# The first layer's first blocks: eight split products or sixteen whole float32 ones

## The chip, the core and the metric

The kernel runs on one core of one Trainium2 chip. The metric is the device time of one execution in microseconds (us); the times shown are those of three runs. TensorE has two clock levels, 1.2 and 2.4 GHz; the profile gives the share that was granted (1.0 is 2.4 GHz).

## What is computed

Two layers over 256 tokens of width 2048, all in float32. Each layer takes a modulation `mod = silu(c) @ w_ada + b_ada` (six vectors of 2048), then a mixer and a feed-forward:

```python
h = rmsnorm(x, g_pre_mix[i]) * (1.0 + sc1) + sh1
z = h @ w_in[i]                       # 2048 x 6608: GLA's q, k, v, g, a and RWKV7's r, k, v, w, a, g
o_gla = gla_mixer(...)                # 8 heads, causal decayed attention
o_rwkv = rwkv7_mixer(...)             # 16 heads, delta rule
y = jnp.concatenate([o_gla, o_rwkv], axis=-1) @ w_out[i]
x = x + gt1 * rmsnorm(y, g_post_mix[i])
h = rmsnorm(x, g_pre_ffn[i]) * (1.0 + sc2) + sh2
y = jnp.square(jax.nn.relu(h @ w_ff1[i])) @ w_ff2[i]
x = x + gt2 * rmsnorm(y, g_post_ffn[i])
```

## The kernel before

Channels lie on partitions: `x` and `h` are 16 k-tiles of 128 channels by 256 tokens. A weight block is 2048 inputs by 128 outputs, 1 MiB; `wtile` (L283) loads it into `wraw` (three buffers of 1 MiB) from SyncE's queue (SP), and `split` (L295) makes of each half two float32r parts: `hi` by a cast on ScalarE, `lo` by a subtraction on VectorE. `h` is split the same way into `hh` and `hl`. A block is then 16 k-tiles of three products (`hi` x `hh`, `hi` x `hl`, `lo` x `hh`), 48 in all (L311 to L313), each 128x128 weights by 256 columns. Smaller products in the mixers are whole float32 ones: one product each of undivided operands.

The modulation is 96 jobs per layer (`ada_job`, L251): load 1 MiB of `w_ada`, multiply by `silu(c)` and sum on VectorE (L256).

The first stage is `first_norm` (L357). For k-tile k it does the two jobs that its scale and shift need, makes `h` of that k-tile (`norm_block`, L434), loads `w8[k]` (the k-th k-tile of eight blocks, 512 KiB), splits it and adds 8 x 3 products (`grow`, L348) to eight accumulators, one in each of the eight PSUM banks. These eight blocks (`FIRST[0]`, L55) are the low-rank columns w, a, g, g and the keys k0 to k3.

Then `mixers` (L899 and on) runs the other blocks of `w_in` in the order of the words in `ORDER[0]` (L68): `kab` two key blocks, `qn` a query and a key block of GLA, `hn` its values, `gn` its gates, `vn` RWKV's r and v of pair n; `T` posts the inverse of the 32 x 32 diagonal blocks (`inverse32`, L605), which needs all keys. Words post chains of dependent small work (`Chains`, L106): at most two are active, and after each quantum (4 k-tiles of a block, 12 products) one step of them is put between. A word outside `EARLY` waits while more than one chain is queued. `v0`'s chain needs `T`; `vn` needs `v(n-2)`. The modulation jobs 32 to 79 are spread over the weight tiles: 48/58 a tile at first, none after the word `R0`, and after `Ra` the rest over 34 tiles, the last 16 of which are `w_out`'s. The banks are `psm` (3), `psx` (3) and `ps2` (a pair), and the first blocks hold all of them until their words are reached.

## Time and profile before

| | us |
|---|---|
| runs: median (lowest to highest) | 2786.74 (2786.28 to 2793.4) |
| span of the profiled execution | 2786.0 |
| TensorE busy in it | 2658.6 |
| VectorE busy in it | 1997.1 |
| ScalarE busy in it | 1421.5 |

The page gives the profiled execution by its span alone; the median of the runs is 0.7 us above it. Busy times of TensorE are those of overlapping records. The rows that are used stand below; times are us from the start of the span.

### The profile page before, as it was taken

Reading aid. Unit: us, or ns where it says so; the run is one execution under the profiler, and the core shown is the slowest. Engines: PE = TensorE matmul, PEld = TensorE weight load, DVE = VectorE, ACT = ScalarE, POOL = GpSimd, SP = SyncE. Lnnn points to the kernel's source line nnn. Section 1 sums busy time; section 2 is a strip of 40 time slices with the busy share of each in tenths; the row PEclk is TensorE's granted clock in tenths of the full one; section 3 lists DMA queues with packets and bytes.
Section 4 is the critical chain, followed back from the end, with each engine's and each line's share of the span. In section 5 each row is a group of like instructions: output and inputs, shape, how many; then the busy total and the mean of one; then the engine's idle time right before and its main releaser. Section 6 shows DMA issues by size and latency. Waiting matters only on the chain.

```text
span 2786.0 us, 55551 instructions
## 1 busy us (share of the span) xinstructions
PE 2658.6 (95%) x23388; PEld 2551.7 (92%) x23388; DVE 1997.1 (72%) x2961; ACT 1421.5 (51%) x2357; POOL 59.2 (2%) x153
## 2 busy tenths in 40 slices
PE   5689999999999999999999999999999999999997
PEld 4678888898999999999988889888989999999997
DVE  8997986678867777777777798655785465565655
ACT  3378644445644434434577875444474443443443
POOL 0000000000000000000001000000000000000000
PEclk8799999999999999999999999998999999999999
DMA  9775576576777777777745547654845666666653
GB/s 402 312 278 196 182 279 239 208 271 231 254 287 289 275 284 284 286 281 282 282 176 206 205 154 264 224 175 159 327 157 212 213 213 218 218 213 212 212 184 119
DMA packets 104082, 659.20 MB, mean 237 GB/s; under 512 B 11540, under 2 KB 20884, under 8 KB 32408
## 3 DMA queue, kind: packets, MB, share of 16 engines
q1 hardware_dynamic: 87848, 618.19, 61.5%
q10 hardware_dynamic: 15984, 37.46, 3.7%
q8 instruction: 183, 3.00, 0.4%
q14 instruction: 67, 0.55, 0.1%
HBM read 638.83 MB, written 16.78 MB: 235 GB/s over the span
## 4 chain that ended last, share of the span: by engine, by line
PE 84%; DVE 9%; DMA 3%; ACT 3%; issue 2%; ACTq 0%; POOL 0%; DVEq 0%; SPq 0%
PE pm L311 14%; PE pm L313 14%; PE pm L312 14%; PE px L312 8%; PE px L313 8%; PE px L311 8%; DVE raw L256 3%; DVE lo L300 2%; PE p L504 1%; DMA raw<-in_wout_dram 1%; PE pm L993 1%; PE pm L994 1%; PE px L451 1%; PE pm L995 1%; ACT hi L299 1%
## 5 line engine op out<-in xcount | busy, mean ns | idle before, releaser
L300 DVE TENSOR_TENSOR lo<-raw,hi 128x1024 fp32r<-128x1024 f32 (+1 forms) x792 | 959.7, 1216 | 544.3 <-ACT hi L299 537.8
L299 ACT CAST hi<-raw 128x1024 fp32r<-128x1024 f32 (+1 forms) x792 | 822.3, 1043 | 800.6 <-PE pm L312 356.1
L311 PE MATMUL pm<-hh,hi 128*128 128x256 f32 x2624 | 762.5, 291 | 3.6 <-ACT hi L299 1.5
L313 PE MATMUL pm<-hh,lo 128*128 128x256 f32 x2624 | 750.4, 286 | 3.9 <-DVE lo L300 3.9
L312 PE MATMUL pm<-hl,hi 128*128 128x256 f32 x2624 | 749.9, 286 | 0.0
L311 PEld LDWEIGHTS pm<-hh,hi 128*128 128x128 f32 x2624 | 504.5, 192 | 14.1 <-issue 2.0
L313 PEld LDWEIGHTS pm<-hh,lo 128*128 128x128 f32 x2624 | 504.9, 192 | 8.9 <-DVE lo L300 5.2
L312 PEld LDWEIGHTS pm<-hl,hi 128*128 128x128 f32 x2624 | 505.4, 193 | 4.6 <-issue 1.6
L256 DVE CUSTOM_DVE_ANT_0 raw<-raw,cond 128x2048 f32<-128x2048 f32 x192 | 439.0, 2287 | 38.3 <-DMA raw<-in_ada_dram 37.8
L313 PE MATMUL pm<-hid,lo 128*128 128x256 f32 x1024 | 289.0, 282 | 0.0
L313 PE MATMUL px<-hid,lo 128*128 128x256 f32 x1024 | 288.3, 282 | 0.0
L312 PE MATMUL px<-hid,hi 128*128 128x256 f32 x1024 | 288.2, 281 | 0.0
L312 PE MATMUL pm<-hid,hi 128*128 128x256 f32 x1024 | 288.0, 281 | 0.0
L311 PE MATMUL pm<-hid,hi 128*128 128x256 f32 x1024 | 287.2, 280 | 0.0
L311 PE MATMUL px<-hid,hi 128*128 128x256 f32 x1024 | 287.1, 280 | 0.0
L313 PE MATMUL px<-hh,lo 128*128 128x256 f32 x896 | 253.6, 283 | 0.0
L311 PE MATMUL px<-hh,hi 128*128 128x256 f32 x896 | 253.5, 283 | 0.0
L312 PE MATMUL px<-hl,hi 128*128 128x256 f32 x896 | 253.5, 283 | 0.0
L311 PEld LDWEIGHTS px<-hid,hi 128*128 128x128 f32 x1024 | 194.5, 190 | 0.0
L311 PEld LDWEIGHTS pm<-hid,hi 128*128 128x128 f32 x1024 | 194.4, 190 | 0.0
L313 PEld LDWEIGHTS pm<-hid,lo 128*128 128x128 f32 x1024 | 193.1, 189 | 0.0
L313 PEld LDWEIGHTS px<-hid,lo 128*128 128x128 f32 x1024 | 193.0, 189 | 0.0
(333 smaller groups left out, 4184.4 us busy)
## 6 DMA issues: line engine op xcount, KB each, us to landing
raw<-in_ff_dram SPq DMA_DIRECT2D x242, 1024.0 KB, 4.9
raw<-in_ada_dram SPq DMA_DIRECT2D x192, 1024.0 KB, 6.2
raw<-in_win_dram SPq DMA_DIRECT2D x90, 1024.0 KB, 5.1
raw<-in_wout_dram SPq DMA_DIRECT2D x32, 1024.0 KB, 5.4
raw<-in_ff1s_dram SPq DMA_DIRECT2D x16, 896.0 KB, 4.6
spill<-pk ACTq DMA_DIRECT2D x16, 640.0 KB, 4.1
pk<-spill ACTq DMA_DIRECT2D x16, 640.0 KB, 5.0
raw<-in_w_dram SPq DMA_DIRECT2D x16, 512.0 KB, 10.5
```

The source lines that it names most:

```text
L256: nc.vector.tensor_tensor_reduce(out=raw, in0=raw, in1=self.cond, op0=ALU.mult, op1=ALU.add, scale=1.0, scalar=0.0, accum_out=self.mod[:, ...
L299: self.nc.scalar.copy(hi, half)
L300: self.nc.vector.tensor_tensor(lo, half, hi.bitcast(F32), op=ALU.subtract)
L311: nc.tensor.matmul(ps, hi[:, n % 8], xh(k), start=n == 0, stop=False)
L312: nc.tensor.matmul(ps, hi[:, n % 8], xl(k), start=False, stop=False)
L313: nc.tensor.matmul(ps, lo[:, n % 8], xh(k), start=False, stop=n == KT - 1)
L451: self.nc.tensor.matmul(ps, self.ones, sq[:, q], start=k + q == 0, stop=k + q == KT - 1)
L504: self.nc.tensor.matmul(v[:, h, n + c], l[hs, cs], r[hs, cs], start=True, stop=True)
L993: nc.tensor.matmul(vps[c], hh[:, kk, cs], hi[:, kq], start=kk == 0, stop=False)
L994: nc.tensor.matmul(vps[c], hl[:, kk, cs], hi[:, kq], start=False, stop=False)
L995: nc.tensor.matmul(vps[c], hh[:, kk, cs], lo[:, kq], start=False, stop=kk == KT - 1)
```

## The change

`FIRST[0]` has sixteen blocks: w, g, g, a, q0's two, k0 to k7, q1's two. Each of the eight banks holds two of them, side by side (256 columns each). They are no longer split: the stage loads `w16[k]` (1 MiB: the k-th k-tile of sixteen blocks, into `wraw`) and multiplies it by `h` itself, one whole float32 product per block and k-tile. Only the first of a bank's two products of k-tile 0 carries the start flag. `hh` and `hl` are still made for the later blocks. `ORDER[0]` takes all of these words first, and `EARLY` names them. `f512`, which now holds `h` for TensorE, has three buffers in this stage; the masks are loaded into a buffer of the modulation's pool. The rest of the diff takes comments out.

```diff
-FIRST = ((WB_W, WB_A, WB_G, WB_G + 1) + tuple(range(WB_K, WB_K + 4)),
+FIRST = ((WB_W, WB_G, WB_G + 1, WB_A, WB_GLA, WB_GLA + 1) + tuple(range(WB_K, WB_K + 8)) + (WB_GLA + 6, WB_GLA + 7),
...
-ORDER = ('k01 k23 q0 h0 g0 k45 q1 k67 R0 h1 P.9 T g1 q2 h2 g2 q3 v0 Ra v1 v2 v3 v4 v5 v6 v7 h3 g3',
+ORDER = ('q0 k01 k23 k45 k67 q1 h0 g0 R0 h1 P.9 T g1 q2 h2 g2 q3 v0 Ra v1 v2 v3 v4 v5 v6 v7 h3 g3',
...
-EARLY = ("k01", "k23")
+EARLY = ("q0", "k01", "k23", "k45", "k67", "q1")
...
-        mf = self.wraw.tile([P, D], F32, name="raw")[:, 0:NMASK]
+        mf = pool.tile([P, D], F32, name="raw", bufs=PRE_BUFS)[:, 0:NMASK]
...
-        first = [self.psm.tile([P, 512], F32, name="pm") for _ in range(3)] + [self.bank() for _ in range(3)]
-        first += [pair[:, n] for n in range(2)]
-        self.first = [(ps[:, :T], True, True) for ps in first]
+        banks = [self.psm.tile([P, 512], F32, name="pm") for _ in range(3)] + [self.bank() for _ in range(3)]
+        banks += [pair[:, n] for n in range(2)]
+        self.first = [(ps[:, n * T:n * T + T], True, True) for ps in banks for n in range(2)]
         for k in range(KT):
             self.ada_job(0, k, pool)
             self.ada_job(0, 16 + k, pool)
-            self.norm_block(pool, 0, rstd, 0, k, 1)
+            h = self.norm_block(pool, 0, rstd, 0, k, 1)
             if k == KT - 2:
-                self.constants()
-            raw = pool.tile([P, D // 2], F32, name="raw8", bufs=3)
-            nc.sync.dma_start(out=raw, in_=self.a["w8"][k])
-            hi, lo = self.split(raw, P)
-            self.grow(hi, lo, self.hh[:, k], self.hl[:, k], k)
+                self.constants(pool)
+            raw = self.wraw.tile([P, D], F32, name="raw")
+            nc.sync.dma_start(out=raw, in_=self.a["w16"][k])
+            w = raw.rearrange("p (n c) -> p n c", c=P)
+
+            for n, (ps, _, _) in enumerate(self.first):
+                nc.tensor.matmul(ps, w[:, n], h[:, 0], start=k == 0 and n % 2 == 0, stop=k == KT - 1,
+                                 skip_group_check=True)
...
-        t = pool.tile([P, n, T], F32, name="f512")
+        t = pool.tile([P, n, T], F32, name="f512", **({"bufs": 3} if n == 1 else {}))
...
+        return t
```

## Rows read from the trace of the kernel before

**Rows 1.** The page's first part: busy us, share of the span, instructions.

```profile
PE 2658.6 (95%) x23388; PEld 2551.7 (92%) x23388; DVE 1997.1 (72%) x2961; ACT 1421.5 (51%) x2357; POOL 59.2 (2%) x153
```

**Rows 2.** Windows: stretch, its length, busy us (instructions) by engine, clock, DMA share, GB/s.

```profile
27.00:132.00 105.00, 69.54 (x383) 65.99 (x384) 101.97 (x166) 32.32 (x52) 3.45 (x1) 0.78 0.89 362
132.00:272.00 140.00, 127.37 (x1331) 116.54 (x1330) 121.31 (x265) 110.12 (x222) 8.74 (x26) 0.97 0.67 236
272.00:330.00 58.00, 52.70 (x606) 50.34 (x605) 51.31 (x130) 37.36 (x57) 2.26 (x6) 0.94 0.50 178
330.00:353.00 23.00, 21.86 (x308) 20.42 (x307) 22.03 (x54) 16.64 (x33) 0.00 (x0) 1.00 0.55 185
353.00:576.00 223.00, 220.88 (x2106) 191.04 (x2104) 155.90 (x216) 100.92 (x224) 11.29 (x18) 1.00 0.67 239
576.00:668.00 92.00, 90.20 (x736) 88.67 (x736) 73.03 (x81) 44.05 (x69) 4.33 (x16) 1.00 0.88 326
```

**Rows 3.** Timeline of VectorE, one k-tile of the first stage: start, duration, instruction.

```profile
98.50 1.23 DVE L300 TENSOR_TENSOR lo<-raw,hi 128x1024 fp32r<-128x1024 f32 x1
99.65 0.42 DVE L444 TENSOR_TENSOR hl<-f,hh 128x256 fp32r<-128x256 f32 x1
...
100.45 2.28 DVE L256 CUSTOM_DVE_ANT_0 raw<-raw,cond 128x2048 f32<-128x2048 f32 x1
...
105.68 1.23 DVE L300 TENSOR_TENSOR lo<-raw,hi 128x1024 fp32r<-128x1024 f32 x1
```

**Rows 4.** Windows of 10 us in the first stage, and SyncE's last issue for it.

```profile
50.00:60.00 10.00, 6.10 (x33) 5.78 (x34) 10.00 (x21) 3.92 (x6) 0.00 (x0) 0.66 1.01 417
...
120.00:130.00 10.00, 6.91 (x38) 6.54 (x39) 8.32 (x14) 4.15 (x7) 1.45 (x1) 0.79 0.06 15
...
106.94 0.33 SPq L372 DMA_DIRECT2D raw<-in_w_dram  x1
```

**Rows 5.** Timeline of TensorE in the first stage; in brackets the idle time before.

```profile
27.58 1.01 PE L353 MATMUL pm<-hh,hi 128*128 128x256 f32 x3 [8.63 <-ACT hh L443]
...
33.93 0.28 PE L353 MATMUL p<-hh,hi 128*128 128x256 f32 x1
...
40.58 1.01 PE L353 MATMUL pm<-hh,hi 128*128 128x256 f32 x3 [4.33 <-ACT hh L443]
...
132.06 0.41 PE L355 MATMUL p<-hh,lo 128*128 128x256 f32 x1
```

**Rows 6.** Timeline of TensorE around four float32 records, and line L518's count.

```profile
141.05 0.28 PE L312 MATMUL pm<-hl,hi 128*128 128x256 f32 x1
141.17 0.60 PE L518 MATMUL px<-th,wsmA 128*128 128x256 f32 x2
141.60 0.59 PE L519 MATMUL px<-al,wsmA 128*128 128x256 f32 x2
141.85 0.47 PE L313 MATMUL pm<-hh,lo 128*128 128x256 f32 x1
142.15 0.28 PE L311 MATMUL pm<-hh,hi 128*128 128x256 f32 x1
...
L518 PE MATMUL px<-th,wsmA x32: 377/379/483, 134.8 to 1581.2; 128*128 128x256 f32 x32
```

**Rows 7.** Groups by line, VectorE, 132 to 350 us: busy, mean ns, idle before.

```profile
L300 DVE TENSOR_TENSOR lo<-raw,hi 128x1024 fp32r<-128x1024 f32 x52 | 63.3, 1223 | 10.7 <-ACT hi L299 10.6
L256 DVE CUSTOM_DVE_ANT_0 raw<-raw,cond 128x2048 f32<-128x2048 f32 x11 | 25.1, 2285 | 2.3 <-DMA raw<-in_ada_dram 2.3
```

**Rows 8.** Four lines, 0 to 640 us: duration min/median/max in ns, first and last start.

```profile
L596 DVE COPY_PREDICATED at<-masks,p x8: 731/736/749, 156.1 to 270.2; 128x512 f32<-128x512 uint8 x8
L618 DVE STREAM_TRANSPOSE o<-o x1: 2111/2111/2111, 275.9 to 275.9; 128x1024 f32<-128x1024 f32 x1
L640 DVE STREAM_TRANSPOSE tn<-o x1: 2032/2032/2032, 325.9 to 325.9; 128x1024 f32<-128x1024 f32 x1
L654 PE MATMUL px<-tn,at x64: 191/191/212, 353.4 to 537.6; 32*32 32x32 f32 x64
```

More of the change, by code (lines that the diff above doesn't have):

```diff
@@ L214, in setup, with constants @@
         self.vmix = self.dram.tile([8, P, T], F32, name="vmix")
-    def constants(self):
+    def constants(self, pool):
         nc = self.nc
@@ L1180, in _pack @@
     a["win"] = np.stack([_pack_win(f["w_in"][i], f["vres_w_down"][i - 1] if i else None) for i in range(L)])
-    a["w8"] = a["win"][0][list(FIRST[0])].reshape(8, P, KT, P).transpose(2, 1, 0, 3).reshape(KT, P, 8 * P)
+    a["w16"] = a["win"][0][list(FIRST[0])].reshape(16, P, KT, P).transpose(2, 1, 0, 3).reshape(KT, P, 16 * P)
     a["wins"] = _by_k(a["win"][1][list(FIRST[1])])
```

## Prediction

> **What bounds the kernel now.** I read the page first: TensorE is busy for 95% of the span, VectorE for 72% [rows 1]. Matmul records overlap, so this doesn't say how full TensorE is; the starts of consecutive records do. Then I cut the touched part into stages [rows 2]: 27 to 132 us is the first stage (modulation, first blocks); 132 to 353 us is the part of the first layer's mixers up to the first `v` pair (I call it stage A); then the `v` pairs, and from 576 us `w_out`. Everything after 668 us is left as it is.
>
> The first stage is paced by VectorE: busy 102.0 of 105 us [rows 2], with one k-tile every 7.18 us (from one `lo` row to the next: 98.50, 105.68) [rows 3]. A k-tile costs it two reductions of 2.28, one `lo` of 1.23, two passes of 0.42 and small ones. The DMA runs full beside it (417 GB/s, share 1.01) until the 16th weight tile is issued at 106.94; then it has nothing left of this stage (share 0.06 from 120 to 130) [rows 4]. TensorE works in bursts with gaps, at a mean granted clock of 0.78 [rows 2].
>
> In stage A no engine is at its end all the time. VectorE is the fullest: 121.3 + 51.3 + 22.0 = 194.6 of 221 us, 88% [rows 2]. TensorE's need is less than its busy time: a quantum of 12 products is 12 x 0.12 = 1.43 us (0.12 from one start to the next, 141.05 to 141.17 [rows 6]). Up to `v0` there are 104 quanta = 149 us, with some 27 us of small float32 products (an estimate from the shapes and the 0.215 below): 80% of 221. The chain through it: the last key block's mask at 270.2, the 32 x 32 inverse from its first transpose at 275.9 to its last at 325.9, the first use of its result at 353.4 [rows 8].
>
> **First stage, after.** Per k-tile, VectorE loses one `lo` (1.23): 7.18 - 1.23 = 5.95 us. ScalarE loses one cast. `hh` and `hl` are still made. So VectorE no longer paces it.
>
> DMA: a k-tile brings 2 MiB of modulation and now 1 MiB of weights, 3.15 MB; at 417 GB/s [rows 4] 7.5 us. The whole stage moves 53 MB (33.6 modulation, 16.8 weights, 2.1 `x`, constants), 127 us, with the start some 130 us. The mixers then load 8 MiB less, so the kernel's bytes stay the same.
>
> TensorE: a whole float32 product leaves two records; the 16 products of L518 show as 32 [rows 6]. Price: after the product at 141.05 (whose 0.12 ends at 141.17) come four such records, one split product (0.12), and the next starts at 142.15: (142.15 - 141.17 - 0.12) / 4 = 0.215 a record, 0.43 a product, each with weights of its own. At half clock the price doubles (0.41 against 0.28 are the durations at the two levels [rows 5]). A k-tile: 16 x 0.43 = 6.9 us at 2.4 GHz, against 24 x 0.12 = 2.9 before. The block itself gets dearer: 16 x 0.43 = 6.9 us whole, 48 x 0.12 = 5.7 us split; the saving is of splits and of place, not of TensorE's work.
>
> The Trainium skill, "FP8 and Floating Point Precision", TensorE Precision Notes, says that true FP32 takes four passes through the array. Were each pass priced as one split product, a product would cost 0.48 and a k-tile 7.6 us, the stage would end some 11 us later, and the result would be about 2771; two records of 0.215 say 0.43, and the row decides.
>
> So DMA (7.5) and TensorE (6.9) are close. TensorE starts at 27.6 as now. The first burst ran at half clock until about 33.9 [rows 5], which loses 3 us; then 16 x 6.9: 27.6 + 3 + 110 = 141. By the DMA: last bytes at 130, then reduction, small passes, `h` (some 4 us), the last 16 products 6.9: 141 too. Now the last one starts at 132.06 [rows 5]. Extension: +8.5 us, bounds +6 to +15.
>
> New waits: SP's load of `w16[k]` waits for a buffer of `wraw`, which is now free only when TensorE is through with `w16[k-3]`; queued behind it on SP are the next two modulation loads. Three tiles ahead are 22 us of loading, so I take nothing; a bubble of 3 us when the first buffers are full is the upper bound, within the range. `f512` holds `h` until its 16 products are done; three buffers cover that. The masks' load (224 KB) goes to a modulation buffer, nothing. Putting two blocks to a bank adds no instruction; L518 and L519 already write two halves of one bank at the price above.
>
> **Stage A, after.** Eight blocks leave (`q0`, `q1`, `k45`, `k67`): 32 quanta, 46 us of TensorE, 16 halves split: 16 x 1.223 = 19.6 us of VectorE [rows 7], and as many casts of ScalarE. Their PSUM reads come at the stage's start in a row, with nothing between: 12 more passes of 0.4 us, covered by the blocks of `h0`.
>
> The modulation jobs shift: 48/58 per weight tile until `R0`; before, 12 tiles come ahead of it, 9 jobs; after, 4 tiles, 3 jobs. Six jobs of 2.29 [rows 7] and a little, 14 us of VectorE, move behind `Ra` (rate 45/34 instead of 39/34). The trace has 11 reductions in stage A [rows 7].
>
> Counting steps in `ORDER`: the last key step comes at quantum 57 either way (56 before), since four key words of 8 steps go one after the other with two chains active, whatever filler runs between. The inverse ends at quantum 72 instead of 69, and `v0`'s chain follows at 73 instead of 105: before, 35 quanta lay between; after, one. So stage A is then set by chains and VectorE, not by the 46 us of TensorE.
>
> VectorE's work: 194.6 - 19.6 - 14 = 161 us. At the 88% of before: 183 us. `v0` starts at 141 + 183 = 324 instead of 353.4: -29.4. Bounds: 97% full, as the first stage shows is possible [rows 2], 166 us, `v0` at 307: -46. Or the chain is exposed: keys take as long as before (140 us [rows 2]), 281, then 50 us of inverse [rows 8], and a few us: 336 to 342, -11 to -17. I take the middle one: the keys lose six reductions but gain one more chain of scores beside them, and the inverse has less against it.
>
> **Afterwards.** In 353 to 668 VectorE is busy 155.9 + 73.0 of 315 us [rows 2]; 14 us more lies in its idle time. In `w_out` 0.18 jobs more per tile make 3 more MB in 92 us: 326 GB/s become 360. If that cover is gone, it is 6 us; I take 2.5.
>
> Sum against the span 2786.0: -29.4 + 2.5 = -27 (the +8.5 is in the 141): 2759. The median of the runs is 0.7 above the span: **2760**.
>
> **Rivals.**
> 1. VectorE packs closer, or blocks of `v` are pulled into the inverse's waits: -36 to -46, 2742 to 2752. For it: 97% in the first stage. Against it: the keys' steps go round between engines. Chance 0.20.
> 2. The inverse takes the place of the blocks: `v0` at 336 to 342, 2772 to 2778, up to 2784 with the worst of `w_out`. For it: one quantum of slack where 35 were. Chance 0.23.
> 3. Slower: the clock. The first stage's mean was 0.78 [rows 2]. At that mean 16 k-tiles of 6.9 are 141 us, the end is at 169, and that eats the gain: the point of decision is about 0.78. At 0.66, the lowest of the 10 us rows [rows 4], it is 195 us, and the kernel about 2813. At half clock throughout, 248 us and 2866. Against it: the clock fell where TensorE had gaps (8.63 and 4.33 us ahead of the bursts at 27.58 and 40.58), and it rose within a burst that went on (0.28 at 33.93 [rows 5]); now it has next to no gaps. Chance 0.09. The Trainium skill, "TensorE: Matmul & The Clock Gate", Part 1, says that the throttled state is the default and sustained activity releases it; the burst at 27.6 agrees, and by that rule the clock stays up here.
> 4. Nothing moves, as another chain takes over: within 0.3%. Chance 0.04.
>
> Forecast (2752 to 2768): 0.44. The range 2741 to 2784 takes in 1, 2 and the forecast. Some 0.3% (8 us) is what a measurement can tell here: faster by more 0.79, within 0.10, slower 0.11.
>
> **What would show it.** Right: first-stage VectorE below 90% busy, DMA share 1.0 to about 130 us, granted clock over 0.9 after 35 us, last first product at about 141 us; the last key mask at 270 to 281, the inverse's end at 310 to 325, `v0`'s first small product near 324; pairs of `v` still 25 us or so apart. Wrong: PE records of 0.43 and more in the first stage (rival 3), or TensorE idle with the inverse on VectorE (rival 2), or the last `v` pair no earlier although `v0` began earlier.

## The result and the profile after

The changed kernel takes 2824.51 us (median of 4 runs, 2821.39 to 2836.57) beside 2786.51 for the kernel before on the same chip: a ratio of 1.0142, 95% interval 1.0121 to 1.0163, 38 us slower. The forecast was 2760, 26 us faster. The profiled execution has a span of 2819.6 us.

The first part of the page and the windows by stage (stretch, length, busy us with instructions per engine, granted clock, DMA share, GB/s) of the changed kernel answer to [rows 1] and [rows 2]. The stages are the first stage, the mixers to the inverse, the inverse, the `v` pairs, and `w_out`:

```profile
PE 2670.0 (95%) x23132; PEld 2548.0 (90%) x23132; DVE 1962.5 (70%) x2929; ACT 1388.6 (49%) x2327; POOL 58.1 (2%) x153
...
26.00:156.00 130.00, 114.79 (x512) 97.49 (x511) 88.96 (x153) 17.32 (x33) 0.28 (x1) 1.00 0.90 358
156.00:330.00 174.00, 147.95 (x1623) 134.10 (x1624) 128.73 (x311) 137.32 (x275) 12.54 (x28) 0.91 0.50 174
330.00:393.00 63.00, 33.00 (x438) 30.34 (x436) 61.09 (x135) 18.79 (x34) 0.11 (x1) 0.77 0.66 244
393.00:609.00 216.00, 211.77 (x1939) 182.46 (x1940) 138.66 (x202) 98.27 (x220) 12.30 (x22) 0.96 0.57 199
609.00:694.00 85.00, 79.56 (x629) 78.49 (x629) 66.50 (x70) 34.31 (x54) 2.94 (x16) 0.96 0.94 353
```

VectorE fell from 97% to 68% busy in the first stage (88.96 of 130) and the clock there is 1.00, both as the change wants. But the stage is 23 us longer, and in the stretch of the inverse (330 to 393) TensorE has work for half the time (33.0 of 63) while VectorE is full (61.1). From the inverse's first transpose to the end of its last, before and then after:

```profile
275.90:327.90 52.00, 46.70 (x555) 44.34 (x554) 50.35 (x127) 31.43 (x51) 1.11 (x2) 0.93 0.48 173
326.80:393.00 66.20, 36.20 (x464) 33.54 (x463) 64.30 (x136) 21.97 (x39) 1.11 (x2) 0.78 0.66 247
```

VectorE is the full engine in both and has 14 us more to do in the changed kernel. Eight reductions of the modulation now lie beside the inverse, where the kernel before has none (groups of VectorE from 326.8 to 393.0):

```profile
L257 DVE CUSTOM_DVE_ANT_0 raw<-raw,cond 128x2048 f32<-128x2048 f32 x8 | 18.3, 2282 | 0.0
```

The events that answer to [rows 8], with two more marks: the last cast of `w_out`'s operand (L1037), and the sum of squares that closes `w_out` (L342). Columns: line, instruction, duration min/median/max in ns, first and last start.

```profile
L377 PE MATMUL p<-f,raw x128: 379/379/379, 32.9 to 155.2; 128*128 128x256 f32 x128
L601 DVE COPY_PREDICATED at<-masks,p x8: 720/731/744, 198.6 to 318.1; 128x512 f32<-128x512 uint8 x8
L623 DVE STREAM_TRANSPOSE o<-o x1: 2115/2115/2115, 326.8 to 326.8; 128x1024 f32<-128x1024 f32 x1
L645 DVE STREAM_TRANSPOSE tn<-o x1: 1881/1881/1881, 391.1 to 391.1; 128x1024 f32<-128x1024 f32 x1
L659 PE MATMUL px<-tn,at x24: 191/236/258, 393.0 to 439.4; 32*32 32x32 f32 x24
L1037 ACT CAST hh<-o x16: 389/406/409, 584.3 to 609.4; 128x256 fp32r<-128x256 f32 x16
L342 PE MATMUL px<-sq,cs x2: 379/431/483, 707.7 to 708.1; 128*128 128x256 f32 x2
```

The kernel before has these two marks at 579.1 and 667.3:

```profile
L1032 ACT CAST hh<-o x16: 387/404/418, 556.0 to 579.1; 128x256 fp32r<-128x256 f32 x16
L341 PE MATMUL px<-sq,cs x2: 379/431/483, 667.3 to 667.6; 128*128 128x256 f32 x2
```

Set beside each other, the starts up to the end of `w_out` split into seven stretches:

| stretch | before | after | difference |
|---|---|---|---|
| start to the last first product | 132.1 | 155.2 | +23.1 |
| to the first key mask | 24.0 | 43.4 | +19.4 |
| to the last key mask | 114.1 | 119.5 | +5.4 |
| to the inverse's last transpose | 55.7 | 73.0 | +17.3 |
| to the first use of the inverse (`v0`) | 27.5 | 1.9 | -25.6 |
| to the last cast for `w_out` | 225.7 | 216.4 | -9.3 |
| to the sum of squares after `w_out` | 88.2 | 98.3 | +10.1 |
| sum | 667.3 | 707.7 | +40.4 |

Behind that mark the first feed-forward takes 750.4 us before and 750.5 after; the second layer's mixers 603.1 and 596.0, though nothing in them was changed; the rest 765.2 and 765.4. The mixers of the second layer scatter from 591 to 610 us over all the profiled executions below, so a single span says less than the median of the runs. The mark after `w_out` leaves that scatter out, but it too comes from one execution of each kernel.

The eight blocks did leave: behind the first stage TensorE is busy for 29.5 us less, up to the mark. But it is idle for 46.8 us more (552.1 - 482.4 = 69.7 in place of 534.8 - 511.9 = 22.9). The 384 products that left are 46 us at 0.12; busy time fell by less, and the granted clock of this stretch is 0.92 in place of 0.99. Windows from the end of the first stage to the sum of squares, the kernel before first:

```profile
132.50:667.30 534.80, 511.88 (x5075) 466.57 (x5075) 422.70 (x742) 308.59 (x599) 26.13 (x65) 0.99 0.68 245
```

and the kernel after:

```profile
155.60:707.70 552.10, 482.38 (x4691) 434.74 (x4690) 404.32 (x726) 295.87 (x589) 28.17 (x66) 0.92 0.62 223
```

The first stage itself can be read line by line. Timelines of SyncE, VectorE, ScalarE and TensorE around one k-tile (start, duration, instruction, in brackets the idle time before it and what ended it):

```profile
95.85 0.33 SPq L373 DMA_DIRECT2D raw<-in_w_dram  x1
104.68 0.33 SPq L373 DMA_DIRECT2D raw<-in_w_dram  x1
...
100.64 2.28 DVE L257 CUSTOM_DVE_ANT_0 raw<-raw,cond 128x2048 f32<-128x2048 f32 x1
...
104.69 0.42 DVE L442 TENSOR_TENSOR f<-x,rs 128x256 f32<-128x256 f32 x1 [1.76 <-PE p L377]
105.03 0.15 DVE L270 TENSOR_TENSOR mod<-mod,par 128x1 f32<-128x1 f32 x1
...
105.41 0.15 DVE L281 TENSOR_SCALAR der<-der 128x1 f32<-128x1 f32 x1
...
105.66 0.60 ACT L444 ACTIVATE f<-f,mod,der 128x256 f32<-128x256 f32 x1 [7.80 <-DVE der L281]
...
97.48 2.86 PE L377 MATMUL pm<-f,raw 128*128 128x256 f32 x12 [1.66 <-ACT f L444]
...
106.31 0.92 PE L377 MATMUL pm<-f,raw 128*128 128x256 f32 x3 [1.66 <-ACT f L444]
```

The period is 8.83 us (97.48 to 106.31). Sixteen products take 6.91 us of it (0.432 each; where TensorE doesn't wait, k-tiles follow each other at 6.91, as e1 shows). The rest is a circle of waits. VectorE's queue has the multiply L442 of a k-tile two further on ahead of the small steps (L270 to L281) of the present one. The multiply writes a buffer of `f512`, of which there are three, and TensorE reads that buffer until the 16 products of the k-tile three earlier are done. So VectorE stands 1.76 us until TensorE is through, then makes `der`, then ScalarE makes `h`, then TensorE, which stood 1.66 us for all that, starts again.

### The profile page after: what moved, and what is told of

Same layout as the page of the kernel before. It is cut to its first block, busy times and chain, and to the rows that moved or that the text cites. A ratio compares the mean times of both kernels' runs of the same rounds, so it can differ in the third digit from the quotient of the medians.

```text
span 2819.6 us, 54944 instructions
## 1 busy us (share of the span) xinstructions
PE 2670.0 (95%) x23132; PEld 2548.0 (90%) x23132; DVE 1962.5 (70%) x2929; ACT 1388.6 (49%) x2327; POOL 58.1 (2%) x153
## 4 chain that ended last, share of the span: by engine, by line
PE 82%; DVE 4%; ACT 2%; DMA 1%; issue 1%; ACTq 0%; POOL 0%; DVEq 0%; SPq 0%
PE pm L312 14%; PE pm L314 14%; PE pm L313 14%; PE px L313 8%; PE px L314 8%; PE px L312 8%; PE p L509 1%; DVE lo L301 1%; PE px L456 1%; PE pm L998 1%; PE pm L354 1%; PE pm L999 1%; PE pm L355 1%; PE pm L356 1%; PE pm L1000 1%
## 5 line engine op out<-in xcount | busy, mean ns | idle before, releaser
L301 DVE TENSOR_TENSOR lo<-raw,hi 128x1024 fp32r<-128x1024 f32 (+1 forms) x760 | 919.9, 1215 | 532.7 <-ACT hi L300 526.1
L300 ACT CAST hi<-raw 128x1024 fp32r<-128x1024 f32 (+1 forms) x760 | 786.2, 1041 | 784.3 <-PE pm L313 343.3
L312 PE MATMUL pm<-hh,hi 128*128 128x256 f32 x2496 | 728.9, 293 | 11.8 <-DVE f L1015 6.3
L314 PE MATMUL pm<-hh,lo 128*128 128x256 f32 x2496 | 717.9, 288 | 8.2 <-DVE lo L301 8.2
L313 PE MATMUL pm<-hl,hi 128*128 128x256 f32 x2496 | 717.1, 287 | 0.0
L312 PEld LDWEIGHTS pm<-hh,hi 128*128 128x128 f32 x2496 | 484.0, 194 | 23.1 <-DVE f L1015 6.9
L314 PEld LDWEIGHTS pm<-hh,lo 128*128 128x128 f32 x2496 | 483.8, 194 | 13.9 <-DVE lo L301 10.0
L313 PEld LDWEIGHTS pm<-hl,hi 128*128 128x128 f32 x2496 | 484.8, 194 | 4.4 <-issue 2.1
```

Source lines behind the costliest of these rows:

```text
L300: self.nc.scalar.copy(hi, half)
L301: self.nc.vector.tensor_tensor(lo, half, hi.bitcast(F32), op=ALU.subtract)
L312: nc.tensor.matmul(ps, hi[:, n % 8], xh(k), start=n == 0, stop=False)
L313: nc.tensor.matmul(ps, hi[:, n % 8], xl(k), start=False, stop=False)
L314: nc.tensor.matmul(ps, lo[:, n % 8], xh(k), start=False, stop=n == KT - 1)
```

## Experiments

The ratio is always to the kernel before in runs on the same chip. "Stage end" is the start of the last first product, "mark" the sum of squares after `w_out`.

**e1: sixteen buffers for h.**

```diff
-        t = pool.tile([P, n, T], F32, name="f512", **({"bufs": 3} if n == 1 else {}))
+        t = pool.tile([P, n, T], F32, name="f512", **({"bufs": 16} if n == 1 else {}))
```

> The changed kernel with one edit: h of the first stage has 16 buffers (f512) instead of 3. Theory A: in VectorE's order the multiply of k-tile k+2 stands ahead of the small modulation steps of k-tile k, and with three buffers it waits for TensorE to end k-tile k-1, so that every k-tile is 6.9 us of products plus 1.9 us of hand-over. Then the period falls from 8.84 to 7.5 us (the loading) or less, the last first product ends near 141 us instead of 155.6, and the span loses 10 to 14 us: some 2807. Theory B: the ring wraw sets the period, as SP's load of w16[k] waits for the products of k-3 with the modulation loads queued behind it. Then the period stays at 8.8 and the span at 2820.

Ratio 1.0105 (1.0059 to 1.015). The weights are issued every 6.91 us and the stage ends at 147.1 in place of 155.2 (SyncE's issues, then the last group of first products):

```profile
97.25 0.33 SPq L373 DMA_DIRECT2D raw<-in_w_dram  x1
104.15 0.33 SPq L373 DMA_DIRECT2D raw<-in_w_dram  x1
...
L377 PE MATMUL p<-f,raw x128: 379/379/379, 33.2 to 147.1; 128*128 128x256 f32 x128
```

The circle of waits was the ring of three buffers. It explains 8 us of the first stage's 23. How much of that reaches the end isn't shown: the mark comes at 708.1 in this execution, as in the changed kernel (707.7), since `w_out` takes 105.2 us in place of 98.3, and the intervals of the two ratios overlap.

**e2: the last two weight tiles in a ring of their own,** so that the mixers' weights find free buffers sooner.

```diff
-            raw = self.wraw.tile([P, D], F32, name="raw")
+            raw = (self.wraw.tile([P, D], F32, name="raw") if k < KT - 2
+                   else pool.tile([P, D], F32, name="raw16", bufs=2))
```

> The changed kernel with one edit: the last two weight tiles of the first stage (k = 14, 15) lie in two buffers of their own instead of wraw. Theory A: the period stays 8.84, but the mixers' first weights and modulation jobs are issued from about 120 us on (140 to 156 now), so that TensorE and VectorE have work right after the last first product: the first key mask comes 8 to 15 us earlier than 198.6, the span loses as much: 2805 to 2812. Rival: the 19 us more between the stage's end and the first key mask come from the twelve PSUM reads in a row and from q0's scores going ahead of the keys; then the first mask moves by less than 4 us.

Ratio 1.015 (1.0104 to 1.0195); the first mask comes 44.4 us behind the stage end (43.4 in the changed kernel). The mixers' first weights are issued at 127.6 in place of 140.0, so the mixers don't start late for want of them. The stage itself ends later, at 160.1: VectorE stands 4.4 us for the masks (1.4 in the changed kernel), and TensorE 4.6 behind it.

**e3: h made in x's own place, and the ring of e2.**

```diff
-        t = pool.tile([P, n, T], F32, name="f512", **({"bufs": 3} if n == 1 else {}))
+        t = self.x[:, k:k + n] if n == 1 else pool.tile([P, n, T], F32, name="f512")
```

> Both cures: h is made in place in x (no ring at all, which VectorE could wait for), and the last two weight tiles have buffers of their own. If the two causes add: last first product near 141 us, first key mask at 170 to 178, v0's first small product at 362 to 370, span 2790 to 2800, about the kernel before or 0.4% over it. If the mixers' chains are the only bound (keys 119 us, inverse 75 us, then 213 us of v pairs), the whole shift of the first mask is kept to the end: 25 us of 33.6.

Ratio 1.0095 (1.0063 to 1.0127), stage end 145.0. It cures the same as e1. The first mask still comes 45.7 us behind, and the mark at 705.3.

**e4: as e3, and the inverse at its own priority** (`LATE` puts the inverse's passes back behind other work on VectorE).

```diff
-LATE = (150, 60)
+LATE = (0, 60)
```

> As the one with both cures, and the 32 x 32 inverse of the first layer no longer put back by 150 places (LATE 0). Theory: after the change the inverse has one quantum of slack, and the 75 us that it takes (50 before) stand on the path; at its own pace it needs some 40 us (62 passes of 0.34, transposes, copies), so v0 comes 25 to 35 us earlier than in the run with both cures and the span is 2760 to 2772, below the kernel before. Rival: the inverse then pushes the splits of h2, g2, q3 back on VectorE, TensorE waits for these, and the span moves by less than 8 us.

Ratio 1.0067 (1.0044 to 1.009). From the first transpose to the last the inverse takes 58.9 us; in e3 64.1, after 64.3, before 50.0. Windows over the inverse, e3 first:

```profile
317.00:383.00 66.00, 35.30 (x455) 32.46 (x453) 64.20 (x136) 21.82 (x39) 1.12 (x3) 0.79 0.68 248
```

and e4:

```profile
311.00:372.00 61.00, 37.60 (x444) 34.76 (x444) 54.59 (x129) 21.43 (x40) 1.17 (x3) 0.79 0.54 199
```

In both TensorE idles for a third to a half of it: nothing is left to cover the inverse. Beside e4's inverse lie five reductions in place of e3's eight. The intervals of the two ratios overlap; the mark comes at 689.6.

**e5: the kernel before with the same number,** the control for e4 (the same line changed).

> The kernel before with one number changed: the 32 x 32 inverse keeps its own priority (LATE 0 in place of 150). It is the control for the run with both cures and the same number, where the inverse took 59 us in place of 64 and the span fell by 15. If that gain belongs to the changed kernel alone (there the inverse stands alone between the keys and v0, with nothing to cover it), the kernel before moves by less than 3 us: its inverse takes 50 us already and v0 comes 27 us behind it. If the number is simply better, the kernel before gains as much, 10 to 15 us (2772 to 2776).

Ratio 1.0016 (0.9999 to 1.0033). What e4 gained belongs to the changed kernel alone: the inverse is shorter here too (45.4 us in place of 50.0), but `v0` starts at 354.1 as before (353.4), so with blocks beside the inverse its length costs nothing.

**e6: the kernel before without the eight blocks,** its first stage untouched. The 384 products and the splits of `q0`, `q1`, `k45` and `k67` are left out, and what is computed from them with them.

```diff
+            if i == 0 and (WB_K + 4 <= b < WB_K + 8 or b in (WB_GLA, WB_GLA + 1, WB_GLA + 6, WB_GLA + 7)):
+                ps = self.psm.tile([P, 512], F32, name="pm")[:, :T]
+                nc.tensor.matmul(ps, self.ones, self.cond[:, :T], start=True, stop=True)
+                return ps
             return (yield from self.block_steps(
```

> The kernel before, its first stage untouched, without the products and splits of the eight blocks (q0, q1, k45, k67): their PSUM tiles get one product of constants each. So the mixers lose what the change takes out of them, and nothing is paid for it in the first stage. Theory of step 1 (the stage up to v0 is VectorE's work at 88%): 121 us of VectorE up to the last key mask become some 88, the last mask comes at 232 to 245 in place of 270, v0 near 315, the kernel near 2750. Theory now (the keys are four chains one after the other, whatever stands between): the eight masks still take 110 to 120 us, the last comes at 262 to 275, the inverse takes longer than 50 because words with modulation now lie beside it, v0 comes at 325 to 345, the kernel at 2755 to 2775.

Ratio 0.9915 (0.9882 to 0.9947): some 21 to 24 us, of the 46 us of TensorE that the blocks were worth, with nothing paid for them. Its masks and its window from the stage end to the mark:

```profile
L596 DVE COPY_PREDICATED at<-masks,p x8: 720/732/749, 166.5 to 261.4; 128x512 f32<-128x512 uint8 x8
...
132.50:658.20 525.70, 482.54 (x4706) 431.95 (x4706) 401.17 (x725) 292.95 (x582) 20.10 (x64) 0.96 0.65 233
```

`v0` starts at 323.3, 30 us earlier than before, yet the mark comes only 9 us earlier in this execution (658.2 against 667.3). TensorE does the same 482.5 us of work as in the changed kernel and idles 43.2. Both theories missed part of it: the eight masks take 94.9 us, not the 110 to 120 of the theory by chains, and the last comes at 261.4, not at 232 to 245 as by VectorE's work. The gain up to `v0` is handed back behind it: 3 us among the `v` pairs, where TensorE is full (224.7 of 228.5 us), and 18 in `w_out`, which takes 106.4 us and in which TensorE idles 15.

**e7: as e4, the keys first.** `k01` and `k23` come ahead of `q0`, and the load of the gates' first weights (`wsmA`) goes ahead of the PSUM reads on ScalarE.

```diff
-ORDER = ('q0 k01 k23 k45 k67 q1 h0 g0 R0 ...
+ORDER = ('k01 k23 q0 k45 k67 q1 h0 g0 R0 ...
-            nc.scalar.dma_start(out=wsm, in_=self.a["wsm"][i, j, :, 0:3])
+            with self.tc.high_priority(300 if i == 0 and j == 0 else 0):
+                nc.scalar.dma_start(out=wsm, in_=self.a["wsm"][i, j, :, 0:3])
```

> Both cures and the inverse at its own priority (the run before it, span 2799), and in addition the keys first: k01 and k23 ahead of q0 in the order, and the load of the first pair's small weights put ahead of the twelve PSUM reads on ScalarE. If the way from the end of the first stage to the first mask (42 us against 24 before) is what the early blocks cost, the first mask comes at 165 to 172 in place of 187, the masks take 114 to 118 again, the last comes at 282 to 288, v0 at 350 to 358 and the span falls by 14 to 20, to 2780 to 2785. If VectorE's work up to the last mask is the bound (139 us behind the stage's end), the last mask stays at 295 to 302 and the span at 2793 to 2799.

Ratio 1.0033 (1.0016 to 1.0051), some 10 us less than e4; the mark comes 13 us earlier (676.5). But the first mask comes only 4 us earlier (183.0), 36.3 us behind the stage end, and the last at 297.5; the rest of the gain lies between the last mask and the end of the inverse (52.5 us, with four reductions beside it). Neither theory foresaw that.

**e8: as e7, the rest of the modulation two words later.**

```diff
-... v0 Ra v1 v2 v3 ...
+... v0 v1 v2 Ra v3 ...
```

> As the run with the keys first, with the rest of the modulation started two words later (Ra behind v2 in place of v0), so that no reduction lies beside the inverse. If the five reductions (11 us) and their splits lengthen the inverse, it takes 50 us in place of 59, and the span falls by 6 to 10 more, to 2770 to 2777. If the inverse's own chain of small VectorE passes sets it, or the reductions put off are missed later, nothing moves by more than 3 us.

Ratio 1.0098 (1.0067 to 1.0129), some 18 us worse than e7. Three reductions still lie beside the inverse (four in e7), and three `lo` passes more, so the run hardly tests its first theory: the inverse takes 53.5 us, as in e7. The mark comes 5 us later than in e7 and the feed-forward takes 757.1 us, 7 more. `w_out` has 18 reductions in place of 15 and takes 108.8 us (99.5 in e7), so the work put off seems to be missed there.

**e9: as e7, 1.5 steps of the chains per quantum** until the inverse is posted.

```diff
-ORDER = ('k01 k23 q0 k45 k67 q1 h0 g0 R0 h1 P.9 T g1 q2 ...
+ORDER = ('P1.5 k01 k23 q0 k45 k67 q1 h0 g0 R0 h1 T g1 P.9 q2 ...
```

> As the run with the keys first, with 1.5 steps of the chains after each quantum of products (1.0 before) until the inverse is posted and 0.9 after that: counted in the order, the last key word ends after 32 quanta and 47 steps of the chains in place of 55 quanta and 55 steps. If the keys go by the chain's steps (2.5 to 2.9 us a step in every run so far, however many products lie between), the last mask comes 47 x 2.77 = 130 us behind the first stage's end, at 275 in place of 297; the inverse has blocks beside it, v0 comes at 335 to 345 and the span at 2768 to 2776, below the kernel before. If they go by the quanta of TensorE between the steps, the last mask comes at 235 to 250 and v0 is set by the 72 quanta. If VectorE's total up to v0 is the bound (179 us of 214 in the run before), v0 stays at 352 to 359 and the span does not move.

```profile
L603 DVE COPY_PREDICATED at<-masks,p x8: 722/733/746, 179.4 to 269.1; 128x512 f32<-128x512 uint8 x8
```

Ratio 1.0012 (0.9991 to 1.0033), no longer to be told from the kernel before, nor by the intervals from e7. The last mask comes at 269.1 in place of 297.5, nearest to the theory by steps, and `v0` at 323.9. That is 35 us earlier than in e7, but the last cast and the mark come only 10 us earlier (567.2 against 577.0): behind `v0` there are now 243 us of work to the last cast, where e7 has 218. No reduction lies beside the inverse, which takes 43.7 us.

**e10: as e7, the lo parts among the keys on GpSimd.**

```diff
-        self.nc.vector.tensor_tensor(lo, half, hi.bitcast(F32), op=ALU.subtract)
+        eng = self.nc.gpsimd if self.lo_pool else self.nc.vector
+        eng.tensor_tensor(lo, half, hi.bitcast(F32), op=ALU.subtract)
```

> As the run with the keys first, with the lo parts of the splits of h0, g0, h1, g1, q2 and h2 on GpSimd in place of VectorE (same values, same order): some 24 of the 30 lo passes ahead of the last mask, 29 us of VectorE's 121, lie on an engine that is idle there. If VectorE's work holds the keys, the last mask comes 20 to 30 us earlier (268 to 277). If the steps of the chain hold them, the last mask moves by less than 8 us (290 to 300), as the passes on VectorE were in its gaps; later if a lo on GpSimd takes several times 1.2 us and the products wait for it.

Ratio 1.0078 (1.0052 to 1.0105); the last mask comes 18 us later. The run doesn't tell the theories apart, since VectorE wasn't relieved: a `lo` takes 2.6 us on GpSimd, and some passes of VectorE beside it stand as long (the last section shows it).

**e11: the kernel before with the pace of e9,** the control for it.

> The kernel before with the same pace (1.5 until the inverse is posted): the control for the run with the pace on the changed kernel. There eight blocks more lie between, and VectorE is at 97.7 + 22.2 = 120 us of 138 up to the last mask. If the pace helps only where the chains are exposed, nothing moves by more than 5 us here (span 2780 to 2792). If the pace is simply better, the last mask comes at 255 or before and the span falls by as much as in the changed kernel.

Ratio 1.0036 (1.0019 to 1.0054): slower by 10 us. There is no trace of it that can be set beside the others, so the times alone speak: what the pace seems to give in the changed kernel (e9), it costs here.

**e12: as e9, twelve first blocks** (`q0` and `q1` go back to the mixers).

```diff
-FIRST = ((WB_W, WB_G, WB_G + 1, WB_A, WB_GLA, WB_GLA + 1) + tuple(range(WB_K, WB_K + 8)) + (WB_GLA + 6, WB_GLA + 7),
+FIRST = ((WB_W, WB_G, WB_G + 1, WB_A) + tuple(range(WB_K, WB_K + 8)),
...
-ORDER = ('P1.5 k01 k23 q0 k45 k67 q1 h0 g0 R0 h1 T g1 P.9 q2 ...
+ORDER = ('P1.5 k01 k23 k45 k67 q0 h0 g0 R0 q1 h1 T g1 P.9 q2 ...
...
```

The first blocks then need six banks in place of eight, and a k-tile loads 0.75 MiB.

> As the run with the pace, with twelve first blocks in place of sixteen: q0 and q1 go back to the mixers as split blocks, behind the keys' words. Per k-tile of the first stage 2 + 0.75 MiB are 2.88 MB, 6.9 us at 417 GB/s in place of 7.5, and TensorE needs 12 x 0.432 = 5.2 us in place of 6.9: the stage ends at 134 to 138 in place of 145. In the order the last key word ends after 40 steps of the chains in place of 47, so at 2.5 to 2.8 us a step the last mask comes 100 to 112 us behind the stage's end, at 235 to 250 (269 in the run before); TensorE has 23 us of products more to do behind the stage. If the stage and the keys set the time, w_out's sum of squares comes 10 to 20 us earlier than in the run before (653.7), at 634 to 644, and the kernel at 2768 to 2780, faster than before. If TensorE's work behind the first stage sets it, what the stage gives back is taken by the four blocks and the kernel stays within 5 us of the run before (2784 to 2793).

Ratio 1.0031 (1.0011 to 1.0051). Its stage ends with that of the kernel before (133.1 against 132.1), its last mask comes at 257.4 and its inverse ends at 310.9, 13 and 15 us earlier than before. And `v0` starts at 353.3, where it started before (353.4): the products still to be done seem to set it, 42 us behind the inverse's last transpose, and the mark comes 9 us later.

**e13: eight blocks whole,** the kernel before with its own blocks, order and mixers, and whole products in the first stage. Two things come along: `f512` has six buffers there, and the masks go to the modulation's pool, as in the change.

```diff
-        mf = self.wraw.tile([P, D], F32, name="raw")[:, 0:NMASK]
+        mf = pool.tile([P, D], F32, name="raw", bufs=PRE_BUFS)[:, 0:NMASK]
...
-            hi, lo = self.split(raw, P)
-            self.grow(hi, lo, self.hh[:, k], self.hl[:, k], k)
+            w = raw.rearrange("p (n c) -> p n c", c=P)
...
+            for n, (ps, _, _) in enumerate(self.first):
+                nc.tensor.matmul(ps, w[:, n], h[:, 0], start=k == 0, stop=k == KT - 1)
...
-        t = pool.tile([P, n, T], F32, name="f512")
+        t = pool.tile([P, n, T], F32, name="f512", **({"bufs": 6} if n == 1 else {}))
```

> The kernel before with whole float32 products for its own eight first blocks (one to a bank, as before), order and mixers untouched: one part of the change alone. Per k-tile VectorE loses the lo pass (7.18 becomes 5.95), TensorE needs 8 x 0.432 = 3.5 us, and 2 + 0.5 MiB are 2.62 MB, 6.3 us at 417 GB/s, which now paces the stage. 16 k-tiles are 0.9 us shorter each, all but the first few: the stage ends at 121 to 126 in place of 132.5. If the mixers are bound by chains and products that both start at the stage's end, everything moves up by that: w_out's sum of squares at 652 to 658 in place of 663.4, the kernel at 2774 to 2781, faster than before by 0.2 to 0.4%. If the mixers need the loads of their weights first, which stand behind those of the stage, the first mask comes no earlier than 156 and the kernel stays at 2784 to 2789.

Ratio 1.0026 (1.0011 to 1.0041): not faster but slower, and the stage ends at 138.5 in place of 121 to 126. VectorE, one late k-tile:

```profile
101.14 2.28 DVE L257 CUSTOM_DVE_ANT_0 raw<-raw,cond 128x2048 f32<-128x2048 f32 x1
...
103.55 2.29 DVE L257 CUSTOM_DVE_ANT_0 raw<-raw,cond 128x2048 f32<-128x2048 f32 x1
...
106.26 0.15 DVE L281 TENSOR_SCALAR der<-der 128x1 f32<-128x1 f32 x1
107.58 0.42 DVE L447 TENSOR_TENSOR hl<-f,hh 128x256 fp32r<-128x256 f32 x1 [1.16 <-ACT hh L446]
107.92 2.29 DVE L257 CUSTOM_DVE_ANT_0 raw<-raw,cond 128x2048 f32<-128x2048 f32 x1
```

The period is 6.78 us (101.14 to 107.92), not 5.95. With the `lo` gone VectorE stands 1.16 us for ScalarE's `hh`, which nothing fills now. The multiply of `x`, which ran ahead through the six buffers, is missing in this k-tile. The kernel before has one without it too, and needs 6.73 us for it (`lo` to `lo`):

```profile
120.05 1.23 DVE L300 TENSOR_TENSOR lo<-raw,hi 128x1024 fp32r<-128x1024 f32 x1
...
126.78 1.23 DVE L300 TENSOR_TENSOR lo<-raw,hi 128x1024 fp32r<-128x1024 f32 x1
```

So of the 1.23 us removed nothing is won. Besides, it stands 3.4 us for the masks and does splits of the mixers' weights before the last k-tiles. And the first mask comes 35.9 us behind the stage end, where the kernel before needs 24.

**e14: as e12, at the old pace** of one step per quantum.

```diff
-ORDER = ('P1.5 k01 k23 k45 k67 q0 h0 g0 R0 q1 h1 T g1 P.9 q2 ...
+ORDER = ('k01 k23 k45 k67 q0 h0 g0 R0 q1 h1 P.9 T g1 q2 ...
```

> As the run with twelve blocks whole, with one step of the chains per quantum up to the inverse in place of 1.5. Counted in the order, the last key word ends after 48 quanta and 47 steps (28 quanta and 40 steps in the run before), so TensorE has 20 quanta more among the keys and as many fewer behind them. If the pace starved TensorE early (its clock 0.83 among the keys) and piled the products up later, TensorE's idle time from the stage's end to w_out falls from 42 to some 25 us, w_out's sum comes at 655 to 662 in place of 672.7, and the kernel at 2776 to 2786. If products taken out are simply replaced by idle time, as chains and products must end together, the sum comes at 662 to 675 again and the kernel at 2786 to 2796.

Ratio 0.9985 (0.9968 to 1.0003), 11 us less than e12 by the pace alone, with the mark at 664.8. The clock among the keys is 0.96 (0.83 in e12). With more of the filler left, the slower pace is the better one. TensorE's idle time to the mark is 39 us, not the 25 expected.

**e15 and e16: the masks in a tile of their own,** loaded at the beginning; e15 with the twelve blocks of e14, e16 with the sixteen of e9.

```diff
-        mf = pool.tile([P, D], F32, name="raw", bufs=PRE_BUFS)[:, 0:NMASK]
-        nc.scalar.dma_start(out=mf, in_=self.a["msk"])
...
+        self.mf = pool.tile([P, NMASK], F32, name="mf", bufs=1)
+        nc.scalar.dma_start(out=self.mf, in_=self.a["msk"])
```

> As the run with twelve blocks at the old pace, with the masks loaded into a tile of their own at the beginning of the first stage. VectorE stood 4.6 us for them at 113 to 118. If TensorE's last products follow VectorE's steps there, the stage ends 3 to 4.5 us earlier (at 130 in place of 134.3) and the kernel at 2776 to 2780, faster than before by 0.2 to 0.35%. If the DMA sets the end of the stage, the stage ends at 134 again and the kernel stays at 2780 to 2784.

> As the run with all cures and sixteen blocks (keys first, pace 1.5), with the masks loaded into a tile of their own at the beginning. TensorE stood 4.4 us behind VectorE for them. If TensorE's 6.9 us per k-tile set the stage, the stage ends at 140 to 142 in place of 145, and the kernel at 2783 to 2786. If the DMA sets its end, nothing moves by more than 2 us.

The wait to be removed, VectorE in e14 and then TensorE in e3:

```profile
117.89 0.39 DVE L229 CAST masks<-raw 128x448 uint8<-128x448 f32 x1 [4.59 <-DMA raw<-in_msk_dram]
```

```profile
129.75 4.44 PE L378 MATMUL pm<-x,raw 128*128 128x256 f32 x12 [4.42 <-ACT x L445]
```

Both stages end earlier by that: e15 at 129.9 in place of 134.3, e16 at 141.0 in place of 145.5. The kernels: 0.998 (0.9964 to 0.9995) and 1.0002 (0.9984 to 1.002), in both within their predecessors' intervals. The cure of the stage is shown; that it reaches the end isn't.

**e17 and e18: the modulation back ahead of the inverse;** e17 from e15, e18 from e16.

```diff
-... q0 h0 g0 R0 q1 h1 P.9 T ...
+... q0 h0 g0 q1 h1 R0 P.9 T ...
```

```diff
-... q1 h0 g0 R0 h1 T ...
+... q1 R1.5 h0 g0 h1 R0 T ...
```

> As the run with twelve blocks and the masks' own tile, with the modulation going on at its first rate until the inverse is posted (four weight tiles, q1 and h1, later): 8 jobs before the inverse in place of 4 or 5, as many as in the kernel before (9). If the jobs put off are what lengthens w_out, it takes 88 to 92 us with 12 or 13 reductions in place of 100 with 14, and its end comes at 662 to 667 in place of 671.9, unless the reductions now lengthen the keys (8 us of VectorE at most); the kernel at 2776 to 2781. If w_out is longer for another reason (its operand ready sooner, its weights not yet loaded), it stays at 98 to 102 and the kernel at 2782 to 2786.

> As the run with all cures, sixteen blocks and the masks' own tile, with 1.5 jobs a weight tile over h0, g0 and h1 (9 jobs before the inverse in place of 3). If the jobs put off are what lengthens w_out, it takes 88 to 92 us in place of 103; six reductions (14 us) lie among the keys instead, where VectorE is some 78% busy, so the last mask comes 0 to 10 us later (265 to 275), and w_out's end at 656 to 665 in place of 665.7; the kernel at 2778 to 2786. If w_out is longer for another reason, the kernel comes out at 2787 to 2797.

Ratios 0.9986 (0.9971 to 1.0001) and 0.9984 (0.9965 to 1.0003). In e17 `w_out` still takes 100.5 us, with 13 reductions that stand 11.5 us for their loads; in e18 it takes 90.4, but its operand is ready 12 us later, and the mark comes at 664.9 in place of 665.7. The reductions of VectorE in `w_out`'s stretch (count, busy us, mean ns, idle time before them), e17:

```profile
L255 DVE CUSTOM_DVE_ANT_0 raw<-raw,cond 128x2048 f32<-128x2048 f32 x13 | 29.7, 2287 | 11.5 <-DMA raw<-in_ada_dram 11.5
```

the kernel before:

```profile
L256 DVE CUSTOM_DVE_ANT_0 raw<-raw,cond 128x2048 f32<-128x2048 f32 x12 | 27.4, 2285 | 0.0
```

So with 13 reductions each `w_out` takes 100.5 us in e17 and 90.4 in e18: the number of jobs put off alone doesn't set its length. It goes with it elsewhere: 88 to 91 us in the three traces with 12 reductions (the kernel before, e5 and e13), 98 to 109 with 14 to 18. What holds e17's loads stays open.

## Why the prediction was wrong, point by point

**TensorE's price was right.** 0.43 a product was worked out, 0.432 measured, at a granted clock of 1.00. The Trainium skill, "FP8 and Floating Point Precision", TensorE Precision Notes, speaks of four passes; priced by the split product they would be 0.48, and the trace disagrees with that price.

**Rival 3 (the clock) did not come.** The clock is 1.00 from 26 to 156 us, where it was 0.78 before. The Trainium skill, "TensorE: Matmul & The Clock Gate", Part 1, has sustained activity release the throttle; the trace agrees. What it shows beyond the forecast is the other side: in the stretches where TensorE then had gaps the clock fell to 0.91 and 0.77.

**The first stage: 155.2 in place of 141.** The step that failed is "`f512` holds `h` until its 16 products are done; three buffers cover that". They cover it in count, not in order: VectorE's queue is in program order, so a multiply for the k-tile after next blocks the small steps of the present one (e1, 8 us). "The masks' load goes to a modulation buffer, nothing" failed too. The load stands behind that buffer's last reader and comes in the 15th k-tile: VectorE waits 1.4 us for it in the changed kernel, 4.4 in e2, 3.9 in e3 (cured in e15 and e16). With both cured, the stage with sixteen blocks ends at 141.0, which is the sum's 141. That three tiles of `wraw` are enough was right (in e1 a k-tile takes TensorE's own 6.91 us).

**VectorE's 5.95 a k-tile** was a subtraction of a pass from a period. In e13, the only run where VectorE can show it, a k-tile without the multiply takes 6.78, where the kernel before needs 6.73 for one: the pass removed had covered a wait for ScalarE, and the subtraction won nothing.

**Stage A: 237.8 us from the stage end to `v0`, in place of 183.** This is the step that turned the sign. I took VectorE's work, 161 us, and divided it by the share of before, 88%. Neither held: VectorE is busy for 190 us of 237, 80%. The groups of `lo` passes and reductions that answer to [rows 7], from 155.6 to 393.0:

```profile
L301 DVE TENSOR_TENSOR lo<-raw,hi 128x1024 fp32r<-128x1024 f32 x44 | 53.3, 1221 | 16.9 <-ACT hi L300 16.8
L257 DVE CUSTOM_DVE_ANT_0 raw<-raw,cond 128x2048 f32<-128x2048 f32 x12 | 27.4, 2284 | 4.1 <-DMA raw<-in_ada_dram 2.4 <-issue 1.7
```

The sum counts on 36 and 5 of them (52 - 16, 11 - 6). Splits and jobs of later words moved up into the stretch, so the work ahead of `v0` is no fixed amount. Nor does one engine bound it: up to the last mask VectorE is busy for 120 us of 163 (121 of 139 before), and only beside the inverse is it full. The keys, then the inverse, then `v0` are one chain, and three things lengthened it:
- The first mask comes 43.4 us behind the stage end (24.0 before). "12 more passes of 0.4 us, covered by the blocks of `h0`" looked at TensorE; the reads and table loads stand in ScalarE's queue ahead of the load for the gates, which is issued at 165.8 (128.4 before, ahead of the stage end). With that load at 147.1 and the keys first, 5 us came back (e7, 36.3; e4, 41.7). There is a part that isn't the order's: e13 has the order and blocks of before and needs 35.9. Its raw weights and `h` stay in memory until TensorE's last product, and the mixers' tiles lie in that memory. GpSimd's first memset for the mixers shows it, in the kernel before (released by VectorE 4 us ahead of the stage end) and then after (released by TensorE's last product):

```profile
128.55 3.53 POOL L920 MEMSET at<- 128x4096 f32 x1 [127.28 <-DVE hl L444]
```

```profile
155.72 3.52 POOL L925 MEMSET at<- 128x4096 f32 x1 [154.46 <-PE p L377]
```

  No run tried that by itself, and it isn't the whole either: e6, with the first stage of before, needs 34.4. There, as in the changed kernel, `q0` is at hand from the beginning, and its scores take every other step of the chains. How the 19 us divide among these stays open.
- The keys take 119.5 us (114.1 before). As the prediction counted, as many quanta lie among their steps as before, since the order fills the place of the blocks that left with others. With 1.5 steps per quantum the last word needs 47 steps in place of 55, and they take 89.7 (e9).
- The inverse, 64 us in place of 50. VectorE's work beside it grew by as much, 50.4 to 64.3 us: 18.3 for the eight reductions, less two `lo` passes and some small ones. They are jobs of the part behind `Ra`, to which the order moved six more. I had put those six into VectorE's idle time behind `v0`, but reductions of that part now come beside the inverse, where VectorE is full and nothing covers it. In every trace VectorE is at least 89% busy from the first transpose to the last. With the inverse at its own priority it takes 58.9 us with five reductions (e4), 52.5 with four (e7) and 43.7 with none (e9). No run moves the reductions alone.

I had counted one quantum of slack in place of 35, and the count was right (the first use starts as the last transpose ends). But of my two bounds I took the one by VectorE's share. Rival 2, "the inverse takes the place of the blocks", is the mechanism that came, with its sign (TensorE busy for 36.2 of the inverse's 66.2 us). Its `v0` at 336 to 342 was 51 us too early even at its late end: 14 in the first stage, 23 from there to the last key mask (163 us, where it took the 140 of before), and 14 in the inverse.

**What a removed product is worth.** Even with nothing paid for them, the eight blocks bring 21 to 24 us, not 46 (e6). Up to `v0` the chain is the bound, so TensorE idles (24 of 191 us in e6). From `v0` to the last cast TensorE is the bound, and starting `v0` earlier can only move products behind it: in e9 that stretch grows from 226 to 243 us. In e6 it grows by 3, and `w_out` by 18. In e12 twelve blocks whole cost 1 us in the first stage and bring nothing. Of the 29 us that e6 takes off TensorE's busy time up to the mark, 20 come back as idle time (43.2 in place of 22.9).

**Afterwards: +10.1 us in `w_out`,** where I took 2.5 and at most 6. The count was right: 15 reductions in place of 12. The reductions stand 5.8 us for their loads (none before), and TensorE 6 us for the splits. The `v` pairs, for which I took nothing, won 9.3.

**The account.** From 1.0142 the cures lead to 1.0105 (ring), 1.0067 (inverse's priority, with `h` in place), 1.0033 (keys first), 1.0012 (pace) and 1.0002 (masks). The intervals of neighbours overlap, so the single steps are not told apart; the whole way, from 1.0121 at least to 1.002 at most, is shown. So with every cure found, sixteen whole blocks are worth as much as eight split ones, though the order and the pace are then no longer those of the change: 9 us more in the first stage (141.0 against 132.1), and about as much won behind it. With the modulation moved as well it is 0.9984, with an interval up to 1.0003. With twelve blocks at the old pace the ratio is 0.998 to 0.9986, and the interval of one of these three kernels (e15, 0.9964 to 0.9995) excludes 1. That is less than the 0.3% that I called the least that can be told, and one interval among so many that misses 1 by 0.0005 can be luck. That a form of the change is faster than the kernel before is not shown.

## What to carry to other kernels

Work taken from an engine is worth its full price only in a stretch where that engine is the bound: list the chain's marks (here masks, inverse, first use) with their distances before pricing what lies between them, since much of the filler that is removed from beside a chain comes back as idle time (20 of 29 us in e6). Ask of work that is put off where it will land: here it landed beside the one part of the chain that fills its engine. When an operand gets a longer-lived reader, look at the queue of the engine that refills its buffer, for what stands behind the refill in program order, and at whatever is to reuse its memory next. And subtract a pass from a period only after finding which wait that pass covers.

## What the runs showed of the hardware

In e10 a `lo` of 128 x 1024 takes 2.60 us on GpSimd (1.22 on VectorE), and passes of VectorE beside it are held up. First GpSimd's group with its mean, over the whole execution, then one such pair:

```profile
L303 POOL TENSOR_TENSOR lo<-raw,hi 128x1024 fp32r<-128x1024 f32 x24 | 62.0, 2596 | 161.2 <-ACT hi L301 159.2 <-PE p L868 1.6 <-POOL lo L303 0.2
...
193.13 2.35 POOL L303 TENSOR_TENSOR lo<-raw,hi 128x1024 fp32r<-128x1024 f32 x1
...
193.20 2.43 DVE L832 TENSOR_TENSOR f<-f,o 128x128 f32<-128x128 f32 x1
```

A pass of 128 x 128 that else takes 0.28 us took 2.43 and ended 0.15 us behind GpSimd's. The Trainium skill, "SBUF — State Buffer", Terms, says that the two engines share a port pair that is locked for a whole instruction, so the loser stands still; these rows agree with it. So the idle GpSimd was no free engine here for passes with two inputs beside a busy VectorE.
